# A trunk of split-float matmuls: the low weight half of each feature-major block's first half-group is written 192 bytes further on

## The chip, the cores and the metric

The kernel runs on one core of one Trainium2 chip. The metric is the device time of one execution in microseconds (us). The median of three runs of the kernel before is 890.74 us, the lowest 888.15, the highest 892.55.

## The reference

The reference is a decoder trunk of two layers over 256 positions and a model width of 2048, in float32:

```python
def reference(x, norm_g, final_g, ab_w_in, ..., cd_w_out):
    h = x.astype(jnp.float32)
    ...
    for l in range(DEPTH):                       # DEPTH = 2
        hn = rmsnorm(h, norm_g[l])
        if l % 2 == 0:
            h = h + ab_layer(hn, ...)            # windowed attention + gated linear attention
        else:
            h = h + cd_layer(hn, ...)            # S5 state space groups + HGRN2 heads
    return rmsnorm(h, final_g).astype(x.dtype)
```

Each layer is one wide input projection (`h @ w_in`), the mixers on slices of its result, a SiLU gate, and one output projection (`y @ w_out`). Layer 1 has one more projection inside (`y @ w_glu`). Most of the arithmetic is in these projections, and the change concerns how their weights lie in on-chip memory.

## The kernel before

**Projections.** A projection is cut in blocks of 512 output features. The weights of a block come in groups of 512 input rows (`raw`, one DMA of 1 MB for a group, on SP's queue). `load_split` handles a group in two half-groups of 256 rows (two "k tiles" of 128 rows each). For each half-group ScalarE rounds the weights to the matmul's reduced float format (`wh`, the high half, L168) and VectorE forms what is left (`wl = raw - wh`, the low half, L169). Both tiles are 128 partitions x 4096 bytes and have three buffers. The activations are split in the same manner: `xh`, `xl` for the normed input and `yh`, `yl` for the gated output. A product is then three matmuls: high x high, high x low, low x high.

There are two forms of the block. In the feature-major form, `gemm_fm`, the weights are the stationary operand: each k tile takes twelve matmuls (L181), four with `wh` and `xh`, four with `wh` and `xl`, four with `wl` and `xh`. Each loads 128 x 128 weights (512 bytes of each partition) and streams 256 columns of activations. A block of four groups has sixteen k tiles, so 192 matmuls. In the token-major form, `gemm_tm`, the activations are stationary and 512 columns of weights stream (L200). The last block of the program (L758) has activations stationary and 256 columns of weights; for its second half the weights lie in the freed buffers of `xh` and `xl`.

The program has 22 feature-major blocks. In what follows they are numbered 0 to 21 in order of time: 0 to 7 are in layer 0's input projection, 8 to 11 are layer 0's output projection (with `yh`, `yl`), 12 to 17 are layer 1's input projection, 18 and 19 the projection inside layer 1 (half as long, 96 matmuls), 20 and 21 layer 1's gate. Between and inside the blocks stand small matmuls of the mixers: attention (L415, L431, L435), linear attention (L287, L308, L316, L339), the state space part (L583, L627) and the transposes of gated heads (L504).

**Where the tiles lie.** The pools are laid out one behind the other in each partition. By the addresses of the built program `xh`, `xl`, `yh` and `yl` begin at 0 modulo 512 bytes; `raw` and all buffers of `wh` and `wl` begin at 320 modulo 512. Every stationary slice of 128 weights is 512 bytes long, so all slices of a tile have the tile's own remainder.

**Order.** A scheduler sets the order on each engine from priorities and a timeline of its own; tiles with fewer buffers bring more waits and other orders. `finish_norm` (twice in the program, for `r0` and `r1`) puts the reciprocal norm of each token on all partitions: for each half `t` of the tokens VectorE writes a diagonal matrix `dg` (L126) and TensorE multiplies it with ones (L127); ScalarE copies the result to `rb` (L129). `rb` scales the blocks' results on their way out of PSUM (L359 and L548 among others). `dg` has two buffers. In `finish` of the state space part `ys` and `gw` have a buffer each.

Of the kernel before, what the change touches and what calls it, by code (L numbers as in the profile page):

```python
# [12 lines left out]
F32 = mybir.dt.float32  # L13
F32R = mybir.dt.float32r
# [6 lines left out]
S = 256  # L21
# [36 lines left out]
def trunk(ctx: ExitStack, tc: tile.TileContext, I, out):  # L58
# [4 lines left out]
    stream = ctx.enter_context(tc.tile_pool(name="stream", bufs=6))  # L63
# [4 lines left out]
    small = ctx.enter_context(tc.tile_pool(name="small", bufs=2))  # L68
# [3 lines left out]
    def urgent():  # L72
        return tc.high_priority(offset=HI)
# [16 lines left out]
    def pm_tile(name="pm"):  # L90
        return pm.tile([128, 512], F32, name=name, tag="pm")
# [21 lines left out]
    def finish_norm(tag):  # L113
        V.tensor_add(sqa[:, 0:2], sqa[:, 0:2], sqa[:, 2:4])
        V.tensor_add(sqa[:, 0], sqa[:, 0], sqa[:, 1])
        ps = pm_tile()
        for t in range(2):
            T.matmul(ps[:, t:t + 1], sqa[:, 0, t * 128:(t + 1) * 128], ones[:, 0:1], start=True, stop=True)
        ms = small.tile([128, 2], F32, name="nms")
        V.tensor_scalar(ms, ps[:, 0:2], 1.0 / D, EPS, op0=OP.mult, op1=OP.add)  # L120
        rc = const.tile([128, 2], F32, name=tag + "c")
        rsqrt(rc, ms, 2, "nr")
        pb = pm_tile()
        for t in range(2):
            dg = small.tile([128, 128], F32, name="dg")
            V.tensor_scalar(dg, ident, rc[:, t:t + 1], None, op0=OP.mult)  # L126
            T.matmul(pb[:, t * 128:(t + 1) * 128], ones, dg, start=True, stop=True)  # L127
        rb = const.tile([128, S], F32, name=tag + "b")
        A.activation(rb, pb[:, 0:S], AF.Copy)  # L129
        return rc, rb  # L130
# [9 lines left out]
                    for fn in todo:  # L140
                        fn()

    def load_split(src, g):
        raw = stream.tile([128, 4, 512], F32, name="raw", bufs=3)
        first = state["first"]
        state["first"] = first and g < 3
        with urgent():
            if first:
                for a, b in ((0, 1), (1, 2), (2, 3), (3, 4)) if g == 0 else ((0, 2), (2, 4)):
                    xs = slice(NV + (4 * g + a) * S if g + a else 0, NV + (4 * g + b) * S)  # L150
                    load(xv[:, xs], I["xv"][:, xs])
                    for c in (slice(0, 256), slice(256, 512)) if g + a == 0 else (slice(0, 512),):
                        load(raw[:, a:b, c], src[g][:, a:b, c])
                for kt in range(4 * g, 4 * g + 4):
                    split_x(kt, V_NG0)
            else:
                state["load"] = nc.sync.dma_start(raw, src[g])
        if first and g == 3:
            load_consts()
        for half in range(2):  # L160
            wh = stream.tile([128, 2, 512], F32R, name="wh", bufs=3)
            wl = stream.tile([128, 2, 512], F32R, name="wl", bufs=3)
            with urgent():
                for a, b, c, d in (((0, 1, 0, 256), (0, 1, 256, 512), (1, 2, 0, 512)) if first and g == 0
                                   else ((0, 2, 0, 512),)):
                    r = raw[:, 2 * half + a:2 * half + b, c:d]
                    w, l = wh[:, a:b, c:d], wl[:, a:b, c:d]
                    state["wh"] = A.activation(w, r, AF.Copy)  # L168
                    V.tensor_sub(l, r, w)  # L169
            for k in range(2):  # L170
                yield 4 * g + 2 * half + k, wh[:, k], wl[:, k]
            hook()

    def gemm_fm(src, groups, ah, al, mid=None, order=None):
        ps = pg.tile([128, 4, S], F32, name="pg")
        last = groups * 4 - 1
        for i, kt, wh, wl in _iter(src, groups, mid, order):
            for n, (w, a) in enumerate(((wh, ah), (wh, al), (wl, ah))):
                for c in range(4):
                    cs = slice(c * 128, (c + 1) * 128)  # L180
                    state["mm"] = T.matmul(ps[:, c], w[:, cs], a[:, kt],  # L181
                                           start=(i == 0 and n == 0 and c % 2 == 0),
                                           stop=(i == last and n == 2), skip_group_check=True)
        return ps

    def _iter(src, groups, mid, order):
        for n, g in enumerate(order or range(groups)):
            for m, (kt, wh, wl) in enumerate(load_split(src, g)):
                yield 4 * n + m, kt, wh, wl
            if mid and 2 * (n + 1) == groups:  # L190
                mid()
# [37 lines left out]
    def load(dst, src):  # L229
        prev = state.get("load")  # L230
        with tc.issue_after(prev.ins) if prev else ExitStack():
            state["load"] = nc.sync.dma_start(dst, src)
# [6 lines left out]
    w0 = I["w0"]  # L239
    f, q, k = gla_tiles()  # L240
    psq = gemm_fm(w0[0], 4, xh, xl)

    with tc.issue_after(state["wh"].ins):
# [286 lines left out]
    with urgent():  # L530
        rc1, rb1 = finish_norm("r1")
# [6 lines left out]
    sp_ = sp.enter_context(tc.tile_pool(name="s5", bufs=1))  # L538
# [13 lines left out]
    def s5_quarter(qt):  # L552
# [78 lines left out]
            return go  # L631

        def finish():
            ys = sp_.tile([128, 8, 64], F32, name="ys")
            A.activation(ys, t["py"], AF.Copy)
            for g in range(2):
                for s in range(4):
                    (nc.gpsimd if s % 2 else nc.scalar).dma_start(
                        yv[g, s][:, 8 * qt:8 * qt + 8], ys[g * 64 + s * 16:g * 64 + s * 16 + 16])
            yc = sp_.tile([128, 2, S], F32, name="yc")  # L640
            nc.gpsimd.dma_start(yc, s5_y[256 * qt:256 * qt + 256].rearrange("(j p) f -> p j f", p=128))
            gw = sp_.tile([128, 2, S], F32, name="gw")
            A.activation(gw, yc, AF.Square)
            A.activation(gw, gw, AF.Copy, scale=0.044715, bias=1.0)
            V.tensor_mul(gw, gw, yc)
            A.activation(gw, gw, AF.Tanh, scale=math.sqrt(2.0 / math.pi))
            A.activation(yc, yc, AF.Copy, scale=0.5)
            for n in range(2):
                V.scalar_tensor_tensor(oT[:, 2 * qt + n].rearrange("p (c s) -> p s c", s=4),
                                       gw[:, n].rearrange("p (s c) -> p s c", s=4), 1.0,  # L650
                                       yc[:, n].rearrange("p (s c) -> p s c", s=4), op0=OP.add, op1=OP.mult)
# [11 lines left out]
    for half in range(2):  # L663
        f, q, k = gla_tiles()
# [87 lines left out]
    for half in range(2):  # L752
        ps = pg.tile([128, 2, 512], F32, name="pg")

        def mms(kt, t, w, l):
            ts_ = slice(t * 128, (t + 1) * 128)
            for n, (w_, a_) in enumerate(((w, yh), (w, yl), (l, yh))):
                T.matmul(ps[:, t, 0:256], a_[:, kt, ts_], w_, start=(kt == 0 and n == 0),  # L758
                         stop=(kt == KT - 1 and n == 2), skip_group_check=True)

        for g in range(2):
            raw = stream.tile([128, 8, 256], F32, name="raw", bufs=3)
            with urgent():
                nc.sync.dma_start(raw, I["wo1l"][half, g])
            for n in range(2):
                k0 = 8 * g + 4 * n
                if half:
                    w, l = xh[:, k0:k0 + 4], xl[:, k0:k0 + 4]
                else:
                    w = stream.tile([128, 4, 256], F32R, name="wh", bufs=3)  # L770
                    l = stream.tile([128, 4, 256], F32R, name="wl", bufs=3)
                with urgent():
                    A.activation(w, raw[:, 4 * n:4 * n + 4], AF.Copy)
                    V.tensor_sub(l, raw[:, 4 * n:4 * n + 4], w)
                for k in range(4):
                    for t in range(1 if half else 2):
                        mms(k0 + k, t, w[:, k], l[:, k])
        if half:
            for t in range(2):
                if t:  # L780
                    for kt in range(KT):
                        mms(kt, 1, xh[:, kt], xl[:, kt])
                with urgent():
                    add_in(res, h2, 3, 256, 256, t, ps[:, t, 0:256], 4)
                    store(t)
        else:
            with urgent():
                for t in range(2):
                    add_in(res, h2, 3, 0, 256, t, ps[:, t, 0:256], 3)
                presum()  # L790
# [348 lines left out]
```

## Time and profile before

| | |
|---|---|
| median of 3 runs | 890.74 us (888.15 to 892.55) |
| time of the profiled execution | 894.61 us |
| its span, first to last instruction | 892.7 us |
| TensorE busy with matmuls | 874.1 us (98%) |
| VectorE / ScalarE busy | 636.0 us (71%) / 473.1 us (53%) |
| granted TensorE clock | 0.996 |
| HBM | 201 GB/s over the span |

Matmuls overlap in the pipeline, so "busy" does not say how fast they follow each other. What matters here is the pace: the time from the start of one matmul to the start of the next. It is read from the chain of work that ended last, where a row gives a stretch's start, its length and how many matmuls it holds, and from the start times of groups in the timeline. The duration of a single matmul (issue to end, modelled) is a second sign, since it differs between the paces.

### The profile page before, as it was taken

How to read it: one execution, taken by the hardware profiler on the slowest of the kernel's cores; microseconds unless marked ns; L12 is line 12 of the kernel's file. 1: busy time of each engine (PE TensorE's matmuls, PEld its weight loads, DVE VectorE, ACT ScalarE, POOL GpSimd, SP SyncE). 2: the span in 40 equal slices, each digit the busy share in tenths (PEclk: the TensorE clock that was granted, in tenths of full speed). 3: DMA queues.
4: the chain of work that ended last, by engine and by line, in shares of the span. 5: the costliest groups of instructions: out<-in, count | busy, mean ns of one | idle time of the engine just before them, and what ended most of it. 6: DMA issues, size and time to landing. Idle time of an engine off the chain costs nothing.

```text
span 892.7 us, 18688 instructions
## 1 busy us (share of the span) xinstructions
PE 874.1 (98%) x7728; PEld 804.5 (90%) x7728; DVE 636.0 (71%) x1197; ACT 473.1 (53%) x715; POOL 54.4 (6%) x106
## 2 busy tenths in 40 slices
PE   8999999999999999999999999999999999999995
PEld 8987899888998899999999999899867899988894
DVE  7987975888869868755575586877977655665562
ACT  7654546665655765644443345455545475444451
POOL 0001100111101101000000001100110000000000
PEclk9999999999999999999999999999999999999998
DMA  9827744777756655555575766754654455544432
GB/s 316 318 99 217 257 159 146 231 253 217 264 193 220 223 179 182 206 189 189 190 270 195 267 211 227 247 192 166 222 170 160 183 189 189 189 171 179 176 136 94
DMA packets 40388, 180.40 MB, mean 202 GB/s; under 512 B 12720, under 2 KB 14256, under 8 KB 22768
## 3 DMA queue, kind: packets, MB, share of 16 engines
q1 hardware_dynamic: 29440, 154.99, 49.5%
q0 software_dynamic: 7984, 22.69, 7.7%
q10 hardware_dynamic: 2880, 1.54, 0.6%
q8 instruction: 60, 0.98, 0.4%
q14 instruction: 24, 0.20, 0.1%
HBM read 166.48 MB, written 12.71 MB: 201 GB/s over the span
## 4 chain that ended last, share of the span: by engine, by line
PE 74%; DVE 8%; ACT 6%; DMA 5%; issue 5%; SPq 0%; POOL 0%; POOLq 0%; DVEq 0%; ACTq 0%
PE pg L181 48%; PE pg L200 17%; DVE wl L169 2%; PE pg L758 2%; DMA tabs<-pc 2%; ACT wh L168 1%; PE pm L287 1%; DMA E<-ed 1%; PE pm L339 1%; DMA s5y<-ys 1%; ACT bb L1021 1%; DMA raw<-in_w_dram 1%; ACT x L1039 1%; PE pm L308 1%; DVE PP L1005 1%
## 5 line engine op out<-in xcount | busy, mean ns | idle before, releaser
L168 ACT ACTIVATE wh<-raw 128x1024 fp32r<-128x1024 f32 (+2 forms) x276 | 287.6, 1046 | 325.0 <-PE pg L181 187.6
L169 DVE TENSOR_TENSOR wl<-raw,wh 128x1024 fp32r<-128x1024 f32 (+2 forms) x276 | 332.6, 1207 | 173.7 <-ACT wh L168 165.0
L181 PE MATMUL pg<-xh,wh 128*128 128x256 f32 x1024 | 162.8, 281 | 1.8 <-ACT wh L168 1.7
L181 PE MATMUL pg<-xl,wh 128*128 128x256 f32 x1024 | 163.8, 280 | 0.0
L181 PE MATMUL pg<-xh,wl 128*128 128x256 f32 x1024 | 163.4, 281 | 0.1
L181 PEld LDWEIGHTS pg<-xh,wh 128*128 128x128 f32 x1024 | 137.4, 188 | 3.7 <-ACT wh L168 3.1
L181 PEld LDWEIGHTS pg<-xl,wh 128*128 128x128 f32 x1024 | 138.0, 188 | 0.8 <-issue 0.3
L181 PEld LDWEIGHTS pg<-xh,wl 128*128 128x128 f32 x1024 | 137.9, 189 | 0.8 <-DVE wl L169 0.3
L200 PE MATMUL pg<-wh,xh 128*128 128x512 f32 x320 | 100.4, 395 | 1.8 <-ACT wh L168 1.8
L200 PE MATMUL pg<-wl,xh 128*128 128x512 f32 x320 | 101.0, 396 | 0.5 <-DVE wl L169 0.4
L200 PE MATMUL pg<-wh,xl 128*128 128x512 f32 x320 | 101.0, 395 | 0.0
L200 PEld LDWEIGHTS pg<-wh,xh 128*128 128x128 f32 x320 | 59.3, 188 | 14.8 <-ACT wh L168 2.2
L200 PEld LDWEIGHTS pg<-wl,xh 128*128 128x128 f32 x320 | 59.5, 188 | 14.1 <-DVE wl L169 1.3
L200 PEld LDWEIGHTS pg<-wh,xl 128*128 128x128 f32 x320 | 59.9, 188 | 12.8
L181 PE MATMUL pg<-yh,wh 128*128 128x256 f32 x320 | 50.8, 281 | 0.0
L181 PE MATMUL pg<-yl,wh 128*128 128x256 f32 x320 | 50.6, 281 | 0.0
L181 PE MATMUL pg<-yh,wl 128*128 128x256 f32 x320 | 50.6, 281 | 0.0
L181 PEld LDWEIGHTS pg<-yl,wh 128*128 128x128 f32 x320 | 43.4, 190 | 0.1
L181 PEld LDWEIGHTS pg<-yh,wh 128*128 128x128 f32 x320 | 43.2, 189 | 0.1
L181 PEld LDWEIGHTS pg<-yh,wl 128*128 128x128 f32 x320 | 43.1, 189 | 0.0
L967 POOL DMA_DIRECT2D tabs<-pc x44 | 23.8, 546 | 167.0 <-DVE x L977 43.7
L200 PE MATMUL pg<-wh,yh 128*128 128x512 f32 x96 | 30.1, 394 | 0.0
(350 smaller groups left out, 994.0 us busy)
## 6 DMA issues: line engine op xcount, KB each, us to landing
raw<-in_w_dram SPq DMA_DIRECT2D x100, 1024.0 KB, 5.0
raw<-in_wo_dram SPq DMA_DIRECT2D x28, 1024.0 KB, 4.8
tb<-tabs POOLq DMA_DIRECT2D x8, 768.0 KB, 6.4
tabs<-pc POOLq DMA_DIRECT2D x20, 256.0 KB, 5.7
raw<-in_wg_dram SPq DMA_DIRECT2D x4, 1024.0 KB, 4.8
raw<-in_wo1l_dram SPq DMA_DIRECT2D x4, 1024.0 KB, 4.8
raw<-in_w_dram SPq DMA_DIRECT2D x6, 512.0 KB, 7.4
tabs<-pc POOLq DMA_DIRECT2D x24, 128.0 KB, 4.9
```

Of the source, the lines that this page charges most:

```text
L168: state["wh"] = A.activation(w, r, AF.Copy)
L169: V.tensor_sub(l, r, w)
L181: state["mm"] = T.matmul(ps[:, c], w[:, cs], a[:, kt], start=(i == 0 and n == 0 and c % 2 == 0), stop=(i == last and n == 2), skip_group_c ...
L200: state["mm"] = T.matmul(ps[:, t], a[:, kt, ts_], w, start=(i == 0 and n == 0), stop=(i == last and n == 2), skip_group_check=True)
L287: T.matmul(ps[32 * b:32 * b + 32, t, hd], k[:, hd, r], Q[:, hd, r], start=True, stop=True)
L308: T.matmul(ps[j0:j0 + h, hd, j0 + h:j0 + 2 * h], k[:, hd, b:b + h], Qp[:, hd, b + h:b + 2 * h], start=True, stop=True)
L339: T.matmul(ps[:, (hd - h0) * dv:(hd - h0 + 1) * dv], AT[:, hd, t + j], v[:, j, hd * dv:(hd + 1) * dv], start=(j == 0), stop=(j == t))
L758: T.matmul(ps[:, t, 0:256], a_[:, kt, ts_], w_, start=(kt == 0 and n == 0), stop=(kt == KT - 1 and n == 2), skip_group_check=True)
L967: nc.gpsimd.dma_start(tabs[qt, dst, n], t[src].rearrange("p a b -> p (a b)"))
L1005: V.scalar_tensor_tensor(PP[half[1 - g], g].rearrange("p a b c -> p (a b c)"), x1[half[g]], -1.0, x2[half[g]], op0=OP.mult, op1=OP.subtract)
L1021: A.activation(bb[half[g ^ n], g], z[n][half[g]].unsqueeze(2).to_broadcast([64, 8, 4, 16]), AF.Copy)
L1039: A.activation(v8(x1)[:, r_], cst[:, C_ID64:C_ID64 + 64], AF.Copy, scale=vec[:, V_D + 8 * qt + r_:V_D + 8 * qt + r_ + 1])
```

## The change

`wl` gets buffers of 4608 bytes instead of 4096, and a view into them. In the first half-group of each feature-major block the view begins 48 floats (192 bytes) into the buffer, that is at 0 modulo 512; everywhere else, and in all token-major blocks, it begins at the buffer's start, at 320 modulo 512 as before. A half-group has two k tiles, so 8 of a block's 192 matmuls have a stationary operand at another remainder. 1536 bytes more are needed for this; 512 come back since `dg` has one buffer now, and `ys` and `gw` share one.

```diff
-            dg = small.tile([128, 128], F32, name="dg")
+            dg = small.tile([128, 128], F32, name="dg", bufs=1)
...
-    def load_split(src, g):
+    def load_split(src, g, aside=False):
...
             wh = stream.tile([128, 2, 512], F32R, name="wh", bufs=3)
-            wl = stream.tile([128, 2, 512], F32R, name="wl", bufs=3)
+            o = 48 if aside and half == 0 else 0
+            wl = stream.tile([128, 1024 + 128], F32R, name="wl", bufs=3)[:, o:o + 1024].rearrange("p (k n) -> p k n", n=512)
...
-        for i, kt, wh, wl in _iter(src, groups, mid, order):
+        for i, kt, wh, wl in _iter(src, groups, mid, order, True):
...
-            for m, (kt, wh, wl) in enumerate(load_split(src, g)):
+            for m, (kt, wh, wl) in enumerate(load_split(src, g, aside and n == 0)):
...
-            ys = sp_.tile([128, 8, 64], F32, name="ys")
+            ys = sp_.tile([128, 8, 64], F32, name="ys", tag="ysgw")
...
-            gw = sp_.tile([128, 2, S], F32, name="gw")
+            gw = sp_.tile([128, 2, S], F32, name="gw", tag="ysgw")
...
-                    l = stream.tile([128, 4, 256], F32R, name="wl", bufs=3)
+                    l = stream.tile([128, 1024 + 128], F32R, name="wl", bufs=3)[:, 0:1024].rearrange("p (k n) -> p k n", n=256)
```

All tiles behind `wl` move by 1536 or 1024 bytes, so their remainders modulo 512 stay. Line numbers behind the added line are higher by one (L169 is L170, L181 is L182, L548 is L549).

The single buffer of `dg` moves instructions in two places, one for each `finish_norm`. The order on POOL and SP stays as it was; on TensorE, VectorE and ScalarE only these two places and the 50 us behind the first differ. In the second, TensorE's order in block 12 was this before (L127 is the product with the diagonal matrix):

```order
L181 MATMUL pg<-xl,wh 128x256 x4
L127 MATMUL pm<-dg,ones 128x128 x2
L181 MATMUL pg<-xh,wl 128x256 x4
L181 MATMUL pg<-xh,wh 128x256 x4
L181 MATMUL pg<-xl,wh 128x256 x4
```

and is this now:

```order
L127 MATMUL pm<-dg,ones 128x128
L182 MATMUL pg<-xh,wl 128x256 x4
L182 MATMUL pg<-xh,wh 128x256 x4
L182 MATMUL pg<-xl,wh 128x256 x4
L182 MATMUL pg<-xh,wl 128x256 x4
L182 MATMUL pg<-xh,wh 128x256 x4
L182 MATMUL pg<-xl,wh 128x256 x3
L127 MATMUL pm<-dg,ones 128x128
L182 MATMUL pg<-xl,wh 128x256
```

The two products stood side by side; now 23 matmuls of the block lie between them. On VectorE the same place read

```order
L103 SCALAR_TENSOR_TENSOR r1c<-nru,r1c 128x2
L126 TENSOR_SCALAR dg<-cst,r1c 128x128 x2
L169 TENSOR_TENSOR wl<-raw,wh 128x1024 x2
L548 TENSOR_TENSOR oT<-pg,r1b 128x256 x4
L169 TENSOR_TENSOR wl<-raw,wh 128x1024 x8
```

and reads now

```order
L103 SCALAR_TENSOR_TENSOR r1c<-nru,r1c 128x2
L126 TENSOR_SCALAR dg<-cst,r1c 128x128
L170 TENSOR_TENSOR wl<-raw,wh 128x1024
L126 TENSOR_SCALAR dg<-cst,r1c 128x128
L170 TENSOR_TENSOR wl<-raw,wh 128x1024
L549 TENSOR_TENSOR oT<-pg,r1b 128x256 x4
L170 TENSOR_TENSOR wl<-raw,wh 128x1024 x8
```

The second `dg` stands behind a `wl`, and must wait until the first product has read the only buffer. In the first `finish_norm`, in block 1, the second product moved from beside the first to behind 32 short matmuls:

```order
L127 MATMUL pm<-dg,ones 128x128
L182 MATMUL pg<-xl,wh 128x256 x2
L182 MATMUL pg<-xh,wl 128x256 x4
L182 MATMUL pg<-xh,wh 128x256 x4
L182 MATMUL pg<-xl,wh 128x256 x4
L182 MATMUL pg<-xh,wl 128x256 x4
L182 MATMUL pg<-xh,wh 128x256 x4
L182 MATMUL pg<-xl,wh 128x256 x4
L182 MATMUL pg<-xh,wl 128x256 x3
L380 MATMUL pm<-glo,wgt 128x256 x4
```

where L380 is the first matmul that needs, through `glo`, the row `r0b` that comes from both products. It stands 29 matmuls behind the second of them.

More of the change, by code (lines that the diff above doesn't have):

```diff
@@ L184, in gemm_fm, with _iter @@
         return ps
-    def _iter(src, groups, mid, order):
+    def _iter(src, groups, mid, order, aside=False):
         for n, g in enumerate(order or range(groups)):
-            for m, (kt, wh, wl) in enumerate(load_split(src, g)):
+            for m, (kt, wh, wl) in enumerate(load_split(src, g, aside and n == 0)):
                 yield 4 * n + m, kt, wh, wl
```

## The prediction

> **What bounds the kernel now.** I read the page first: the busy times, the chain, the costliest groups.
>
> ```profile
> PE 874.1 (98%) x7728; PEld 804.5 (90%) x7728; DVE 636.0 (71%) x1197; ACT 473.1 (53%) x715; POOL 54.4 (6%) x106
> ...
> PE 74%; DVE 8%; ACT 6%; DMA 5%; issue 5%; SPq 0%; POOL 0%; POOLq 0%; DVEq 0%; ACTq 0%
> PE pg L181 48%; PE pg L200 17%; DVE wl L169 2%; PE pg L758 2%; DMA tabs<-pc 2%; ACT wh L168 1%; PE pm L287 1%; DMA E<-ed 1%; PE pm L339 1%; DMA s5y<-ys 1%; ACT bb L1021 1%; DMA raw<-in_w_dram 1%; ACT x L1039 1%; PE pm L308 1%; DVE PP L1005 1%
> ```
>
> TensorE is busy 98% of the span and the feature-major line L181 alone is 48% of the chain. Next the waits of TensorE on other engines, whose longest totals are
>
> ```profile
> PE pg L200 <- ACT wh L168: 1.8, 1, 1.8
> PE pg L181 <- ACT wh L168: 1.7, 3, 0.7
> ```
>
> Almost nothing is waited for, so the time of a feature-major block is its 192 matmuls times their pace. The chain in order of time gives that pace stretch by stretch (start, length, matmuls):
>
> ```profile
> 342.77 122.54 PE pg L181 x1046
> 474.10 35.83 PE pg L181 x316
> 744.10 45.23 PE pg L181 x384
> ```
>
> The second stretch runs at 35.83 / 316 = 113.4 ns a matmul, the third at 45.23 / 384 = 117.8 ns. The instructions, their shapes and the remainders of their addresses are the same in both. So one stream has two paces, 4.4 ns apart. I call them quick and slow. The clock is not the cause: in windows inside the first and the second stretch (busy time and count of TensorE and of its weight loads, then the granted clock, the share of the DMA engines, GB/s) it is 1.00 both times.
>
> ```profile
> 387.00:409.50 22.50, 22.50 (x193) 22.50 (x193) 1.00 0.52 185
> ...
> 476.00:497.00 21.00, 21.00 (x188) 21.00 (x187) 1.00 0.70 243
> ```
> The single matmul's duration tells them apart too; these rows are from the first stretch behind 387 us, from the second and from the third (min/median/max ns, first and last start):
>
> ```profile
> L181 PE MATMUL pg<-yh,wl x124: 280/281/282, 386.8 to 429.6; 128*128 128x256 f32 x124
> ...
> L181 PE MATMUL pg<-xh,wl x104: 275/276/369, 473.9 to 508.3; 128*128 128x256 f32 x104
> ...
> L181 PE MATMUL pg<-xh,wh x120: 280/281/364, 743.9 to 785.3; 128*128 128x256 f32 x120
> ```
>
> 281 ns is the slow pace and 276 the quick one, with hardly a value between. A pace holds until something disturbs the stream. The first stretch shows it: it begins quick and turns slow at one hiccup.
>
> ```profile
> 363.61 0.62 PE L181 MATMUL pg<-yl,wh 128*128 128x256 f32 x4
> 364.06 0.62 PE L181 MATMUL pg<-yh,wl 128*128 128x256 f32 x4
> 364.51 0.62 PE L181 MATMUL pg<-yh,wh 128*128 128x256 f32 x4
> 365.05 0.74 PE L181 MATMUL pg<-yl,wh 128*128 128x256 f32 x4
> 365.63 0.64 PE L181 MATMUL pg<-yh,wl 128*128 128x256 f32 x4
> 366.10 0.64 PE L181 MATMUL pg<-yh,wh 128*128 128x256 f32 x4
> ```
>
> Groups of four start 0.45 us apart up to 364.51 (113 ns a matmul). One group is 0.09 us late, and from 365.63 the distance is 0.47 (117.5 ns), which then lasts 100 us. The other way round, behind an attention product:
>
> ```profile
> 236.41 0.64 PE L181 MATMUL pg<-xl,wh 128*128 128x256 f32 x4
> 236.89 0.62 PE L181 MATMUL pg<-xh,wl 128*128 128x256 f32 x4
> 237.34 0.62 PE L181 MATMUL pg<-xh,wh 128*128 128x256 f32 x4
> ```
>
> Here a group takes 0.48, and the next ones 0.45. A few ns more at one place put the stream on the quick pace. This is what the change can act on.
>
> **The change part by part.**
>
> *The eight matmuls at 0 modulo 512.* The stationary slice and the streamed `xh` (or `yh`) then share the remainder. The trace has that pairing at one place, the end of the last block (L758), where both operands are at 0; just before, the same line streams weights at 320 against a stationary operand at 0:
>
> ```profile
> L758 PE MATMUL pg<-wl,yh x32: 278/279/283, 858.9 to 869.8; 128*128 128x256 f32 x32
> ...
> L758 PE MATMUL pg<-xh,yh x16: 278/284/290, 870.0 to 875.4; 128*128 128x256 f32 x16
> ```
>
> In the first row a matmul of this kind comes every third, so 31 x 3 = 93 steps take 10.9 us: 117 ns. In the second, 15 x 3 = 45 steps take 5.4 us: 120 ns. Equal remainders therefore cost some 3 ns against slow and 7 against quick. 22 blocks x 8 = 176 matmuls: 0.5 us if the stream was slow there, 1.2 if it was quick, and I take 0.9. The entry into the pairing is rougher:
>
> ```profile
> 869.84 0.28 PE L758 MATMUL pg<-wl,yh 128*128 128x256 f32 x1
> 869.96 0.29 PE L758 MATMUL pg<-xh,yh 128*128 128x256 f32 x1
> 870.09 0.28 PE L758 MATMUL pg<-xh,yl 128*128 128x256 f32 x1
> 870.21 0.29 PE L758 MATMUL pg<-xl,yh 128*128 128x256 f32 x1
> 870.33 0.28 PE L758 MATMUL pg<-xh,yh 128*128 128x256 f32 x1
> ```
>
> Steps of 0.12, 0.13, 0.12, 0.12: four steps 0.49 us, against 0.45 for a quick group. At 0.04 us for each of the 44 groups of four (two in each block) the whole price is at most 1.8 us.
>
> *What the eight leave behind.* Each block now holds, in its first two k tiles, two groups that run later than either pace. That is a hiccup of the kind and size that changed the pace at 236.41 (0.48 us for that group, 0.49 for the first of L758's). If the stream comes out of it quick, all slow matmuls from the block's 25th up to the next foreign matmul become quick. I counted these in the timeline, block by block: 117 in block 4, 168 each in blocks 8, 9, 10, 11 and 20, 167 in 21, 72 in block 12, together 1196; the first and third stretches of the chain above hold all but block 4's. Times 4.4 ns that is 5.3 us. In blocks 9 to 12 the matmuls ahead of the first such group would be quick as well, carried over from the block before: 4 x 16 x 4.4 ns = 0.3 us. Stretches behind later interruptions keep what those leave. If the stream comes out slow instead, the quick matmuls from the 25th on are lost: 61, 46, 28, 168, 168, 71, 71 and 71 in blocks 1, 5, 6, 7, 13, 14, 15 and 19, with 33 in blocks 2, 16 and 17, together 717, times 4.4 ns: 3.2 us. The bounds of this term are thus -5.6 and +3.2 us. I take the whole gain, because the direct evidence points there: the step behind equal remainders is longer than in either pace, and after a longer step the rows at 236.41 turn quick. The row at 365.05, a late group that turned the stream slow, is the evidence against; there the group came 90 ns late, not 10 to 40.
>
> A rule of the Trainium skill speaks against this whole term. "TensorE: Matmul & The Clock Gate", Step-by-step, says that the engine has two independent read ports in SBUF, one for the streaming operand and one for the weight load. By it the remainder of the weights would not matter, the eight matmuls would cost nothing and leave nothing, and the sum would be 0. The L758 rows above, 117 and 120 ns for the same instruction, do not agree with it.
>
> *The single `dg`.* These rows show the second norm's place, in block 12:
>
> ```profile
> 470.66 0.48 DVE L126 TENSOR_SCALAR dg<-cst,r1c 128x128 f32<-128x128 f32 x2
> 471.96 1.23 DVE L169 TENSOR_TENSOR wl<-raw,wh 128x1024 fp32r<-128x1024 f32 x1 [0.82 <-ACT wh L168]
> 473.49 0.61 PE L127 MATMUL pm<-dg,ones 128*128 128x128 f32 x4
> 474.66 0.36 ACT L129 ACTIVATE r1b<-pm 128x256 f32<-128x256 f32 x1
> 474.78 1.23 DVE L169 TENSOR_TENSOR wl<-raw,wh 128x1024 fp32r<-128x1024 f32 x1 [1.60 <-ACT wh L168]
> ```
>
> The second `dg` now waits on VectorE for the first product, done about 474.0, and takes half of 0.48 us, so it ends near 474.3. The `wl` queued behind it waited for ScalarE until 474.78 anyway, with 1.60 us idle before it, so nothing is late. TensorE comes to the second product 23 matmuls later, 23 x 0.1134 = 2.6 us, near 476.5: no wait. `r1b` follows near 477, about 2.5 us later than now, and the evacuation of block 12 (L548, VectorE), due at the block's end near 476.1, starts a microsecond later; the `wl` behind it on VectorE gets that microsecond too, which the buffers cover (0.82 and 1.60 us idle before the two `wl` above). PSUM has a second buffer, and block 13 fills it for 21.8 us (192 x 113.4 ns). Cost 0. The first norm is the same with longer cover: 29 matmuls stand between the second product and L380. What the two places can do is change a pace by interrupting the stream once more. Behind the second lies the 35.83 us stretch, quick today; if it turned slow up to the first group of eight in block 13, some 24 matmuls would lose 0.1 us, and its whole 316 matmuls 1.4 us if the group failed to mend it.
>
> *`ys` and `gw` in one buffer.* `gw` is written from `yc`, which is read back from memory after `ys` has been stored, so the new wait is always older than one that exists. Cost 0. *The longer `wl` view* gives VectorE the same 1024 elements; L169's duration stays at 1.23 us.
>
> **Sum.** -5.3 - 0.3 + 0.9 = -4.7 us, against the profiled span of 892.7 us: 888.0 us. The profiled execution's own time is 894.61 us, 1.9 us above its span and 3.9 above the median, so I set the difference against the median: 890.74 - 4.7 = 886.0 us. 0.5% is 4.45 us, about what a measurement of this kernel can tell from no change; the border lies at 886.3.
>
> **The rivals.**
> *The paces stay as they are* (independent operands, or a hiccup too small to matter). For it: two groups of eight in 192 are few, and most hiccups of the trace are larger. Against it: the 117 and 120 ns. Time: 0 to +1.8 us, 890.7 to 892.5, middle 891.6.
> *The eight leave the stream slow.* For it: the late group at 365.05. The place is the 25th matmul of each quick block, the price 4.4 ns for each of 717 matmuls, 3.2 us, and 1.2 us for the eights: 890.74 + 4.4 = 895.1 us. It decides when more than about half of the blocks come out slow: with a share q coming out quick the sum is -5.6 q + 3.2 (1 - q) + 0.9, and that is zero at q = 0.47.
> *More than the counted blocks turn quick.* Stretches behind interruptions may change too, since their start is moved by a few ns; the slow matmuls there, by the same count some 830 of them, are worth 3.7 us. This would give 882.3.
>
> **How the numbers follow.** Quick behind the eights, 0.53: 884.0 to 888.0, and just over half of it lies below 886.3. Paces unchanged, 0.22: 889.5 to 892.5. Slow behind them, 0.15: 892.5 to 896. More than the counted blocks, 0.10: 881.5 to 884. Faster by over 0.5%: 0.10 + 0.29 = 0.39. Slower by over 0.5% (over 895.2): the upper third of the third case, 0.05, and 0.04 for the moved norms, which could leave more stretches slow than I see. Within 0.5%: 0.52. The range that leaves out 2 in 10: 882.5 to 893.5.
>
> **What would show it.** Right: the rows of 387 to 430 us and of 744 to 785 us have a median of 276 instead of 281 ns, and groups of four with `wl` in the first two k tiles of a block stand 0.48 to 0.49 us apart from the next. Wrong: those two stretches keep 281, or 474 to 508 us goes to 281. Also wrong: the groups of eight run at 113 ns, in which case equal remainders cost nothing here; or TensorE waits at L127 or L380.

## The result: 1.2% slower, and the profile after

The changed kernel took 900.32 us (median, 898.23 to 905.13), the kernel before beside it 891.6 us: a ratio of 1.0123, with a 95% interval of 1.0093 to 1.0153. The forecast was 886.0 us. The profiled execution of the changed kernel took 898.23 us, its span is 896.4 us. On its page TensorE is busier, and the chain has the same lines at its head; the share of L201 (L200 before) has grown.

```profile
PE 878.4 (98%) x7728; PEld 807.7 (90%) x7728; DVE 636.3 (71%) x1197; ACT 473.0 (53%) x715; POOL 54.4 (6%) x106
...
PE 84%; DVE 5%; DMA 4%; issue 3%; ACT 3%; SPq 0%; POOL 0%; POOLq 0%; DVEq 0%; ACTq 0%
PE pg L182 48%; PE pg L201 25%; PE pg L759 2%; DVE wl L170 2%; DMA raw<-in_w_dram 2%; PE pm L288 1%; PE pm L340 1%; DMA E<-ed 1%; DMA s5y<-ys 1%; ACT wh L169 1%; PE pm L309 1%; PE pm L416 1%; PE pm L1028 1%; PE pm L584 0%; PE pm L623 0%
```

The chain in order of time answers to the three stretches of before (start, length, matmuls):

```profile
343.20 123.25 PE pg L182 x1046
477.94 34.50 PE pg L182 x293
...
747.74 45.24 PE pg L182 x384
```

They run at 117.8 ns a matmul, all three: 123.25 / 1046, 34.50 / 293, 45.24 / 384. Before, the middle one ran at 113.4. So neither of the two stretches from which the gain was to come turned quick, and the one that was quick turned slow. The single matmul's duration says the same (min/median/max ns, first and last start):

```profile
L182 PE MATMUL pg<-yh,wl x122: 281/281/284, 386.7 to 429.3; 128*128 128x256 f32 x122
...
L182 PE MATMUL pg<-xh,wh x99: 276/281/282, 473.8 to 508.4; 128*128 128x256 f32 x99
...
L182 PE MATMUL pg<-xh,wh x111: 277/281/367, 747.5 to 786.0; 128*128 128x256 f32 x111
```

The place where it happens can be seen in the timeline at the start of block 19, which begins at 734.54:

```profile
734.09 0.62 PE L182 MATMUL pg<-yh,wl 128*128 128x256 f32 x4
734.54 0.62 PE L182 MATMUL pg<-yh,wh 128*128 128x256 f32 x4
735.00 0.62 PE L182 MATMUL pg<-yl,wh 128*128 128x256 f32 x4
735.45 0.64 PE L182 MATMUL pg<-yh,wl 128*128 128x256 f32 x4
735.93 0.64 PE L182 MATMUL pg<-yh,wh 128*128 128x256 f32 x4
736.40 0.63 PE L182 MATMUL pg<-yl,wh 128*128 128x256 f32 x4
```

Groups start 0.45 us apart up to 735.45. That is the first group of the block with `wl` at 0 modulo 512. It takes 0.48 us, as forecast, and behind it the distance is 0.47: the slow pace, up to the end of the block. One wait of TensorE has grown, that on the low weights of the token-major form. The rows give the total in us, the number of waits and the longest, before and after:

```profile
PE pg L200 <- DVE wl L169: 0.4, 2, 0.2
...
PE pg L201 <- DVE wl L170: 2.0, 2, 1.8
```

### The profile page after: what moved, and what is told of

It reads as the page before. It is cut to its first block, busy times and chain, and to the rows that moved or that the text cites. A ratio compares the mean times of both kernels' runs of the same rounds, so it can differ in the third digit from the quotient of the medians.

```text
span 896.4 us, 18700 instructions
## 1 busy us (share of the span) xinstructions
PE 878.4 (98%) x7728; PEld 807.7 (90%) x7728; DVE 636.3 (71%) x1197; ACT 473.0 (53%) x715; POOL 54.4 (6%) x106
## 4 chain that ended last, share of the span: by engine, by line
PE 84%; DVE 5%; DMA 4%; issue 3%; ACT 3%; SPq 0%; POOL 0%; POOLq 0%; DVEq 0%; ACTq 0%
PE pg L182 48%; PE pg L201 25%; PE pg L759 2%; DVE wl L170 2%; DMA raw<-in_w_dram 2%; PE pm L288 1%; PE pm L340 1%; DMA E<-ed 1%; DMA s5y<-ys 1%; ACT wh L169 1%; PE pm L309 1%; PE pm L416 1%; PE pm L1028 1%; PE pm L584 0%; PE pm L623 0%
## 5 line engine op out<-in xcount | busy, mean ns | idle before, releaser
L169 ACT ACTIVATE wh<-raw 128x1024 fp32r<-128x1024 f32 (+2 forms) x276 | 287.6, 1045 | 326.4 <-PE pg L182 189.3
L170 DVE TENSOR_TENSOR wl<-raw,wh 128x1024 fp32r<-128x1024 f32 (+2 forms) x276 | 332.6, 1207 | 173.5 <-ACT wh L169 164.1
L182 PE MATMUL pg<-xh,wh 128*128 128x256 f32 x1024 | 163.7, 281 | 1.8 <-ACT wh L169 1.8
L182 PE MATMUL pg<-xh,wl 128*128 128x256 f32 x1024 | 164.9, 282 | 0.5 <-DVE wl L170 0.4
L182 PE MATMUL pg<-xl,wh 128*128 128x256 f32 x1024 | 164.7, 281 | 0.0
L182 PEld LDWEIGHTS pg<-xh,wh 128*128 128x128 f32 x1024 | 138.5, 189 | 3.7 <-ACT wh L169 3.0
L182 PEld LDWEIGHTS pg<-xh,wl 128*128 128x128 f32 x1024 | 138.7, 189 | 1.7 <-DVE wl L170 0.9
L182 PEld LDWEIGHTS pg<-xl,wh 128*128 128x128 f32 x1024 | 138.6, 189 | 0.5
L201 PE MATMUL pg<-wl,xh 128*128 128x512 f32 x320 | 101.5, 397 | 2.1 <-DVE wl L170 2.0
L201 PE MATMUL pg<-wh,xh 128*128 128x512 f32 x320 | 100.7, 395 | 1.6 <-ACT wh L169 1.6
L201 PE MATMUL pg<-wh,xl 128*128 128x512 f32 x320 | 101.0, 395 | 0.0
L201 PEld LDWEIGHTS pg<-wl,xh 128*128 128x128 f32 x320 | 59.3, 188 | 15.8 <-DVE wl L170 3.1
L201 PEld LDWEIGHTS pg<-wh,xh 128*128 128x128 f32 x320 | 59.2, 188 | 14.8 <-ACT wh L169 2.0
L201 PEld LDWEIGHTS pg<-wh,xl 128*128 128x128 f32 x320 | 59.8, 188 | 13.0
L182 PE MATMUL pg<-yh,wh 128*128 128x256 f32 x320 | 50.9, 281 | 0.0
L182 PE MATMUL pg<-yh,wl 128*128 128x256 f32 x320 | 50.8, 281 | 0.0
L182 PE MATMUL pg<-yl,wh 128*128 128x256 f32 x320 | 50.6, 281 | 0.0
L182 PEld LDWEIGHTS pg<-yh,wh 128*128 128x128 f32 x320 | 43.6, 190 | 0.1
L182 PEld LDWEIGHTS pg<-yh,wl 128*128 128x128 f32 x320 | 43.3, 189 | 0.0
L182 PEld LDWEIGHTS pg<-yl,wh 128*128 128x128 f32 x320 | 43.2, 189 | 0.0
L201 PE MATMUL pg<-wh,yh 128*128 128x512 f32 x96 | 30.1, 395 | 0.0
```

What stands on the lines that cost most here:

```text
L182: state["mm"] = T.matmul(ps[:, c], w[:, cs], a[:, kt], start=(i == 0 and n == 0 and c % 2 == 0), stop=(i == last and n == 2), skip_group_c ...
L201: state["mm"] = T.matmul(ps[:, t], a[:, kt, ts_], w, start=(i == 0 and n == 0), stop=(i == last and n == 2), skip_group_check=True)
```

## The experiments

For every kernel I counted one number from its trace: the **excess**, the sum over the matmuls of the feature-major line of the time from one start to the next less 113.3 ns, interruptions left out. It says in microseconds what the paces cost. The profiled execution of before has 9.3 us of it, that of the changed kernel 13.0. The excess and the wait in the table are those of each kernel's one profiled execution. The executions of one kernel scatter by a few microseconds, so the kernels below were compared by the medians of several runs against runs of the kernel before beside them.

| kernel | edit | excess | wait on `wl` near 90 us | median us | ratio, interval |
|---|---|---|---|---|---|
| before_again | none, before | 4.2 | 0 | 888.45 | 0.9982 [0.9949, 1.0016] |
| after_again | none, changed kernel | 12.9 | 1.7 | 898.6 | 1.0102 [1.0038, 1.0166] |
| layout_only | changed, `wl` stays at 320 | 4.4 | 1.8 | 890.35 | 1.0015 [0.9977, 1.0054] |
| eights_only | changed, two `dg` | 13.4 | 0 | 897.32 | 1.0100 [1.0066, 1.0135] |
| dg_one | before, one `dg` | 4.1 | 1.8 | 892.33 | 1.0037 [1.0011, 1.0064] |
| first_128 | changed, eights at 448 | 3.2 | 1.3 | 887.53 | 0.9988 [0.9972, 1.0004] |
| fm_128 | changed, all feature-major `wl` at 448 | 1.8 | 1.8 | 887.28 | 0.9990 [0.9975, 1.0005] |
| gap_128 | before, all `wl` moved 128 bytes | 1.7 | 0 | 885.96 | 0.9972 [0.9955, 0.9988] |

**The bare stream.** The first kernel leaves the trunk out. It is a stream of 128 x 128 by 256 matmuls with the streamed operand at 0 modulo 512 and stationary slices at any multiple of 32 bytes, in three parts: one remainder alone; four matmuls at a remainder inside a slow stream at 320; and the block's own mixture, eight at 320 (as `wh`) and four at a remainder (as `wl`).

```python
for r in REM:                      # 0, 32, ... 480
    for _ in range(12):
        four(320, mm_320); four(320, mm_320); four(r, mm_mix)
```

> A bare stream of the feature-major matmul (128 x 128 weights loaded, 256 columns streamed from a tile at 0 modulo 512), with no other work, which leaves the trunk out. Phase 1 runs 40 matmuls with weights at each remainder in steps of 32 bytes, up and down; phase 2 puts the stream on 320 behind four matmuls at 0, then four at each remainder r, then 56 at 320; phase 3 repeats eight at 320 and four at r. Theory A, the pace is a matter of the two operands' remainders and of a phase that the stream keeps: 0 gives 119 to 120 ns, 320 gives 113.4 or 117.8, four at 0 leave 117.8 behind them every time, and some remainders leave 113.4. Theory B, the pace comes from other engines' traffic: then all remainders run alike here, within 1 ns.

One remainder alone, the pace was 120.0 ns at 0, 118.3 at 32, 117.8 at 64, 117.2 on one pass and 118.6 on the other at 96, 118.7 at 128, 119.9 to 120.1 at 160, 117.8 at 192, 116.7 at 224, and the same again from 256 on. Put into a slow stream at 320, four matmuls at 0, 32, 64, 256, 288 or 320 left it at 117.8; at any of the other ten they left it at 113.3. In the mixture 0 gave 118.3 ns a matmul (the four themselves 119.5), 64 gave 117.8, 128 gave 114.4, 160 gave 119.4, and 192 gave 113.3 throughout, with the upper half of the map equal to the lower. So 160 is the slowest of the mixture, although four matmuls at 160 had left a stream at 320 quick: what four matmuls leave behind and what they cost themselves are two things. The timeline shows the mixture at 0 and at 192 (L47 is the eight, L56 the four):

```profile
346.93 0.64 PE L56 MATMUL ps<-xm,W 128*128 128x256 f32 x4
347.41 1.11 PE L47 MATMUL ps<-xm,W 128*128 128x256 f32 x8
348.35 0.64 PE L56 MATMUL ps<-xm,W 128*128 128x256 f32 x4
...
449.74 0.62 PE L56 MATMUL ps<-xm,W 128*128 128x256 f32 x4
450.20 1.07 PE L47 MATMUL ps<-xm,W 128*128 128x256 f32 x8
451.10 0.62 PE L56 MATMUL ps<-xm,W 128*128 128x256 f32 x4
```

Twelve matmuls take 1.42 us in the first (118.3 ns), 1.36 in the second (113.3 ns). So four matmuls at 0 did not mend the slow stream: the mechanism on which the forecast rested is missing at the remainder that the change chose. At 96 to 224 it is there.

**The changed kernel with `wl` left where it was.** Same instruction order, buffers and single `dg`; only the offset is gone.

```diff
-            o = 48 if aside and half == 0 else 0
+            o = 0
```

> The changed kernel with the offset set to 0: longer buffers of wl, one buffer of dg, shared ys and gw, the same order of all instructions, but no weights at 0 modulo 512. Theory A, the eights at 0 leave the stream slow and that is the loss: time within 0.5% of the kernel before, 887 to 895 us, blocks 7, 13, 14 with their quick stretches (113.4 ns). Theory B, the moved norms and tiles cost the time: 1.008 to 1.015 times the kernel before, as the changed kernel.

Ratio 1.0015, excess 4.4 us: most of the loss went with the 192 bytes. What is left of it, 1.7 us by the medians, has the size of the wait near 90 us, taken up below; the interval reaches from 0.9977 to 1.0054, so the runs alone would not show it.

**Both kernels once more, unchanged.** The first profile of before looked bad (9.3 us of excess), and I wanted to know what a usual execution looks like.

> The kernel before, unchanged. Theory A with paces drawn anew in each execution: where the profiled execution takes under 891 us, more stretches are quick than in the first profile (the 103 us from 362 to 465 us would be worth 3.8 us); each us under 894.6 is some 230 quick matmuls more. Theory B, the paces are the same in every execution: the same stretches are quick and slow as in the first profile, and the spread of 888 to 892.5 us comes from somewhere else.

> The changed kernel, unchanged. Theory A: behind the eights every block is slow (117.8 ns) in this execution too, and where the time is over 900 us, what is over lies in stretches behind interruptions, or in a lower granted clock. Theory B: some blocks are quick this time, and the time goes with them.

The kernel before, in its second profile (887.94 us, span 886.1):

```profile
340.70 118.58 PE pg L181 x1046
468.06 35.83 PE pg L181 x316
...
737.46 45.23 PE pg L181 x384
```

The first stretch, slow in the first profile (122.54 us), is quick here: 113.4 ns. Blocks 8 to 11, from which I had hoped to win the most, are quick as a rule: the stretch takes 118.57 us in the kernel with `wl` left at 320 and 118.58 in the one with a single `dg` (below). The hiccup in block 8 of the first profile was an accident of that execution. The paces are not drawn anew as a whole, though: the other two stretches are what they were (35.83 and 45.23 us). The changed kernel repeats itself: 898.67 us in its second profile, excess 12.9 against 13.0 us, blocks 7 to 14 and 19 to 21 slow behind their eights both times. The two second profiles differ by 896.8 - 886.1 = 10.7 us, of which the paces are 12.9 - 4.2 = 8.8 (unrounded) and the wait on `wl` 1.7.

**The offset alone.** The changed kernel with two `dg` again, so that the instructions stand in the order of before; the room comes from a smaller pitch of `wl`, and `ys` and `gw` still share a buffer.

```diff
-            dg = small.tile([128, 128], F32, name="dg", bufs=1)
+            dg = small.tile([128, 128], F32, name="dg")
...
-            wl = stream.tile([128, 1024 + 128], F32R, name="wl", bufs=3)...
+            wl = stream.tile([128, 1024 + 64], F32R, name="wl", bufs=3)...
```

> The changed kernel without the part that made room: dg has two buffers again and the matmuls stand in the order of before; the low weight half of the first half-group of each feature-major block still begins at 0 modulo 256. Theory A (the eight matmuls at 0 modulo 256 of each block leave the stream at the slow pace, and the single dg costs a wait of its own): no wait of TensorE on wl of more than 0.6 us between 27 and 107 us, every block slow behind its eights, a total excess over 113.3 ns per matmul of 11.5 to 13 us, time 8 to 10 us above before, 896 to 899 us, ratio 1.008 to 1.011. Theory B (the loss of the change is mostly its reordering by the single dg, and the paces follow it): time within 3 us of before, ratio at most 1.003.

```profile
341.07 123.25 PE pg L182 x1046
473.10 37.10 PE pg L182 x316
...
745.28 45.24 PE pg L182 x384
```

117.8, 117.4 and 117.8 ns: the slow stretches are there without any reordering, and between 27 and 107 us TensorE waits for nothing. Ratio 1.0100: the eights account for most of the change. The excess, 13.4, lies a little above the 11.5 to 13 that were expected. This remainder is 0 modulo 256, since the smaller pitch puts one of the three buffers' views at 256 modulo 512; it makes no difference.

**The single `dg` alone.** The kernel before with that one edit, the weights where they were.

```diff
-            dg = small.tile([128, 128], F32, name="dg")
+            dg = small.tile([128, 128], F32, name="dg", bufs=1)
```

> The kernel before with one buffer for dg in place of two, and nothing else: the weights stay where they were (320 modulo 512), the second norm's first half moves and VectorE's order changes as in the changed kernel. Theory A: a wait of TensorE on wl in the token-major blocks of 1.3 to 1.8 us between 80 and 107 us, paces as in the kernel before, time 1 to 3 us above before, 890 to 892 us, ratio 1.001 to 1.003. Theory B (the reordering is the main loss): ratio 1.008 or more. Rival C: the reordering costs nothing, ratio 1.000 plus or minus 0.001, and no wait on wl above 0.6 us.

Ratio 1.0037 and median 892.33 us, both a little beyond what was expected (1.003 and 892). The paces are those of before (excess 4.1). The wait is there:

```profile
PE pg L200 <- DVE wl L169: 2.1, 2, 1.8
```

VectorE's timeline shows where it is from (start, length; in brackets the idle time before and what ended it):

```profile
79.99 1.23 DVE L169 TENSOR_TENSOR wl<-raw,wh 128x1024 fp32r<-128x1024 f32 x1
...
86.78 0.69 DVE L976 TENSOR_TENSOR pc<-E,pB 128x512 f32<-128x512 f32 x1 [4.90 <-DMA E<-ed]
...
88.69 0.69 DVE L979 TENSOR_TENSOR x<-E,pB 128x512 f32<-128x512 f32 x1
89.29 1.22 DVE L169 TENSOR_TENSOR wl<-raw,wh 128x1024 fp32r<-128x1024 f32 x1
```

and in the second profile of before:

```profile
83.32 1.23 DVE L169 TENSOR_TENSOR wl<-raw,wh 128x1024 fp32r<-128x1024 f32 x1 [0.29 <-ACT wh L168]
...
88.42 0.69 DVE L976 TENSOR_TENSOR pc<-E,pB 128x512 f32<-128x512 f32 x1 [3.77 <-DMA E<-ed]
...
90.84 1.22 DVE L169 TENSOR_TENSOR wl<-raw,wh 128x1024 fp32r<-128x1024 f32 x1
```

VectorE stands still for a transfer of `E` in both. With two `dg` one more `wl` is done before that (83.32), and TensorE lives on it. With one `dg` the order behind the first norm has shifted, that `wl` stands behind the wait and behind four operations on `E`, and comes at 89.29. What TensorE does then:

```profile
88.41 0.33 PE L287 MATMUL pm<-gq,gk 128*32 128x32 f32 x14
90.57 0.74 PE L200 MATMUL pg<-wl,xh 128*128 128x512 f32 x2 [1.84 <-DVE wl L169]
91.14 0.66 PE L200 MATMUL pg<-wh,xh 128*128 128x512 f32 x2
91.60 1.05 PE L200 MATMUL pg<-wh,xl 128*128 128x512 f32 x2
92.46 1.05 PE L200 MATMUL pg<-wl,xh 128*128 128x512 f32 x2
```

Behind the wait eight matmuls run at 427 ns each (from 91.60 to 92.46 two take 0.86 us), against 229 ns for this form elsewhere. The window from 92 to 96 us (busy times, then the granted clock) says why: 0.62 here, while the profiled execution of the changed kernel shows 1.00 in the same window. The 0.62 is a mean: the granted clock is 0.50 from 91.60 to 95.00 us and 1.00 behind that.

```profile
92.00:96.00 4.00, 4.00 (x21) 2.75 (x20) 4.00 (x6) 1.06 (x1) 0.57 (x2) 0.62 0.80 260
```

So this execution lost 1.8 us to the wait and 8 x 0.198 = 1.6 us to the clock. The same was in the profile of the kernel with `wl` left at 320, and not in four other profiles with the wait. That profile (897.65 us, one of the two longest runs of its kernel) has a clock of 0.50 in three stretches of 3.4 us, from 91.6, 118.9 and 658.2 us on, behind idle times of TensorE of 1.77, 2.49 and 2.05 us; only the first of them has to do with the wait on `wl`. Such stretches may be a reason why the runs scatter, since the longest run of a kernel mostly has the lowest mean clock. They are not peculiar to the single `dg`: its runs go from 888.5 to 897.2 us, and those of the kernel before beside it from 886.6 to 895.9, the longest with the lowest mean clock of them, 0.989.

**The remainder that mends.** The changed kernel with the eights at 448, which the map says turn a slow stream quick; then with the low weights of all half-groups of the feature-major form there.

```diff
-            o = 48 if aside and half == 0 else 0
+            o = 32 if aside and half == 0 else 0
```

> The changed kernel with the offset of the first half-group at 128 bytes (448 modulo 512) instead of 192 (0 modulo 512); all instructions and their order are the same. Theory A, the remainder decides in which pace the stream is left: by the map, four matmuls at 448 leave 113.3 ns, so every block is quick behind its first k tiles up to the next interruption, also blocks 20 and 21, which are slow in every trace so far (1.7 us): 886 to 889 us, 0.995 to 1.000 of the kernel before, 10 us under the changed kernel. Theory B, any other remainder in the first half-group disturbs the stream into slow: 1.008 to 1.015, as the changed kernel.

> As the run before, but the low half is written 128 bytes further on in all half-groups of feature-major blocks, so that each k tile has eight matmuls at 320 and four at 448. Theory A: by the map this mixture runs at 113.3 ns and finds back to it from slow within a k tile or two, so the slow stretches behind interruptions go as well: the sum of what matmuls take over 113.3 ns falls from 4.2 us (kernel before, second profile) to under 1.5 us; 884 to 887 us, 0.993 to 0.998. Theory B: 1.008 or more.

Both have the order of the changed kernel, with its wait, and both are level with before at the edge of what can be told (0.9988 and 0.9990). Blocks 20 and 21, slow in every profile of before, are quick: the stretch of 384 matmuls is 43.60 us instead of 45.23 in both. With all `wl` at 448 the excess falls to 1.8 us, where under 1.5 was expected, and the ratio misses the 0.993 to 0.998 that were expected: the wait of 1.8 us is still in it.

**A second map.** The trunk is left out again. Four matmuls at each remainder inside a quick stream at 320; the mixture with the streamed operand moved by 64 or 128 bytes, weights moved as far or not; and remainders that alternate.

> A bare stream again, with no trunk. Phase 1 puts the stream on the quick pace (four at 448, then forty at 320), then four at r, then 56 at 320. Theory A: 0 and 256 turn the quick stream slow (117.8 ns behind them), 192 and 448 leave it quick. Rival: the pace behind four matmuls depends on the pace before, and four at 0 leave a quick stream quick. Phase 2 moves the streamed operand to 64 and 128, with the weights moved as far, or not: if only the difference of the two remainders counts, the moved ones repeat the map (r 192 and 448 at 113.3, others slower) and the unmoved ones do not. Phase 3 changes the remainder with every matmul.

In a quick stream only 0 and 256 leave it slow; the other fourteen leave it at 113.3. The timeline shows 0 and 32, the first two (L52 is the four, L49 the stream behind):

```profile
21.47 0.64 PE L52 MATMUL ps<-xm,W 128*128 128x256 f32 x4
21.95 6.76 PE L49 MATMUL ps<-xm,W 128*128 128x256 f32 x56
28.54 0.63 PE L46 MATMUL ps<-xm,W 128*128 128x256 f32 x4
...
33.57 0.64 PE L52 MATMUL ps<-xm,W 128*128 128x256 f32 x4
34.05 6.51 PE L49 MATMUL ps<-xm,W 128*128 128x256 f32 x56
40.40 0.62 PE L46 MATMUL ps<-xm,W 128*128 128x256 f32 x4
```

Both groups of four take 0.48 us. Behind the first, 56 matmuls take 28.54 - 21.95 = 6.59 us (117.7 ns), behind the second 40.40 - 34.05 = 6.35 (113.4 ns). It is not the length of the late group that decides. With weights and streamed operand moved together the map repeats (113.3 for 192 and 448, 118.3 for 0 and 256); with the streamed operand moved alone it doesn't (117.8 to 120.0). Where that leaves all twelve at one difference, the pace is the one of the first map: 120.0 ns at the difference 0, 117.8 at 192. What counts is the difference of the two remainders modulo 256. Which tile has which difference counts too: eight at a difference of 64 and four at 192 run at 113.3, eight at 192 and four at 64 at 117.8.

**The version that follows from it.** The kernel before, with an unused gap of 128 bytes ahead of the `wl` buffers and one behind them, so that `wl` is at 448 everywhere; two `dg`, no longer buffers of `wl`, and the order of before but for two tiny writes on POOL.

```diff
+            if first and g == 0 and half == 0:
+                gap = stream.tile([128, 32], F32, name="gap", bufs=1)
+                G.memset(gap[:, 0:1], 0.0)
             wl = stream.tile([128, 2, 512], F32R, name="wl", bufs=3)
+            if first and g == 0 and half == 0:
+                gap = stream.tile([128, 32], F32, name="gap2", bufs=1)
+                G.memset(gap[:, 0:1], 0.0)
```

> The kernel before with an unused gap of 128 bytes ahead of the buffers of wl and one of 128 bytes behind them: wl begins at 448 modulo 512 everywhere, in token-major blocks too; dg, ys and gw keep their buffers, and the order of the instructions stays. All tiles behind move by 256 bytes. Theory A, remainders count modulo 256 as in the map: paces as in the run before, 884 to 887 us, and token-major blocks keep 229 ns for each 512 columns. If instead remainders count modulo 512, blocks 8 to 11, whose activations now lie at 256, have another pace.

```profile
339.89 118.58 PE pg L187 x1046
467.02 35.83 PE pg L187 x316
...
736.80 43.60 PE pg L187 x384
```

All three stretches are quick (113.4, 113.4, 113.5 ns). Ratio 0.9972, interval 0.9955 to 0.9988: a little faster than the kernel before, by about the 2.5 us of excess that it removes (4.2 - 1.7), and within what was expected. The tiles behind the gaps moved by 256 bytes, `yh` and `yl` with them, and blocks 8 to 11 run at 113.3 ns all the same, which is the period of 256 again.

## Why the prediction was wrong

*The step that failed: what the eight leave behind.* I let them leave the stream quick (-5.3 and -0.3 us). They leave it slow, in every block where nothing interrupts it later. The evidence that I chose was two late groups: one in L758 with equal remainders, after which nothing of the other kind followed, and one at 236.41 with remainders of 320, after which the stream turned quick. I took the lateness for the cause. The second map shows two groups equally late (0.48 us) with opposite ends; the remainder decides. The row at 365.05 (a late group after which the stream turned slow) already spoke against reading lateness as a cure, and I set it aside for its 90 ns.

*The rival that held, and its size.* The eights leave the stream slow: this had the chance 0.15. Its price was put at 4.4 us, 3.2 for the paces and 1.2 for the eights, and is 8.8. Against the first profile of before alone the excess grew by 13.0 - 9.3 = 3.7 us, so the count fitted the execution that it was taken from. I had counted quick matmuls in one execution, the one in which blocks 8 to 12 happened to be slow. In a usual one they are quick, so there is less to win and more to lose: in blocks 8 to 11 that is 4 x (0.87 - 0.01) = 3.4 us of excess more. The same accident made the gain term (744 of its 1196 slow matmuls are there, and the 117 of block 4 were quick in the repeat too) look large.

*The eights themselves* were right: 120 ns forecast, 119.5 in the mixture.

*The single `dg`* was costed at 0 and costs 1.7 to 1.8 us in the changed kernel's profiles, more where the clock drops behind the wait. The second norm did cost nothing, as worked out: the second `dg` waited 0.73 us for the first product, and TensorE waited at neither product. At the first I followed the second product as far as L380 and stopped. The wait is 40 us further on, on VectorE, whose order behind the norm I had listed as different and did not walk through to the next place where VectorE stands still for a transfer.

*`ys` and `gw` in one buffer* and the longer view: 0, and nothing in the runs speaks against it; no run had them alone. The kernel that has them, a single `dg` and all feature-major `wl` at 448 (excess 1.8, wait 1.8) is 1.3 us above the version with gaps, which has `wl` at 448 alone (excess 1.7, no wait on `wl` there); the wait covers that.

Put together: 888.45 us for the kernel before in its repeat, + 8.8 for paces, + 1.8 for the wait = 899.0, against 898.6 and 900.32 measured.

*The independent ports.* The prediction weighed a rule of the Trainium skill ("TensorE: Matmul & The Clock Gate", Step-by-step), two independent read ports for weights and streaming operand, by which the remainder of the weights would not matter. The maps contradict what the prediction drew from it for the time: with nothing but that remainder changed the same matmul takes 116.7 to 120.0 ns alone, and 113.3 to 119.4 in the mixture. Why it does is open.

## What to carry to other kernels

Read off the paces of a matmul stream from the chain, and look at the addresses of both operands: here the pace went with the difference of the remainders modulo 256 of weights and streamed operand. 0 and 160 were the slow ones to keep away from, and with two thirds of the weights at a difference of 64 and one third at 192 the stream stayed quick; the other way round it did not, so measure the pair that you choose. When room is made by taking a buffer from a small tile, follow each engine's new order to its next long wait, not just to the consumer of that tile. And before a gain is counted from stretches that look slow, profile the kernel a second time; a pace that an accident set in one execution is no reserve.

## What the runs showed of the hardware

- A stream of identical matmuls (128 x 128 by 256 columns) with weights and streamed operand at a difference of 64 modulo 256 has two lasting paces, 113.3 and 117.8 ns. Four matmuls with another remainder switch it. From slow, the differences 96 to 224 modulo 256 switch it to quick; from quick, 0 alone switches it to slow (steps of 32 bytes, one execution for each map). Why the pace lasts is open; the runs show only what switches it.
- Remainders that alternate with every matmul run at 113.3 ns for 320 and 448, but at 120.1 for 0 and 128 (streamed operand at 0): being 128 bytes apart is not enough by itself.
- The granted clock fell to 0.50 for 3.4 us, about a microsecond behind an idle time of 1.84 us, with eight matmuls at 427 instead of 229 ns; behind an idle time of 1.79 us in the changed kernel it stayed at 1.00. The Trainium skill ("TensorE: Matmul & The Clock Gate", Part 1) puts the drop behind an idle window of about 3.4 us that runs free of the program. That the drop is seen behind one of two nearly equal waits fits a window of which only the position differs. That an idle time of little more than half its length was enough does not follow from what the Trainium skill says there, and the 14 short matmuls ahead of it do not explain it: in the kernel with `wl` left at 320 the clock fell to 0.50 at 658.2 us behind 2.05 us of idle time with matmuls of 512 columns directly ahead.
